# A retention layer whose queries and keys lose the norm's factor, with the order of its steps laid out anew

## The chip, the cores and the metric

The kernel runs on one core of a Trainium2 chip. The metric is the device time of one execution in microseconds (us). The engines have these short names: PE is TensorE (matmuls), DVE is VectorE, ACT is ScalarE, POOL is GpSimd and SP is SyncE, which here only issues transfers.

## The reference, cut to what matters

The program is a trunk of two layers over 512 tokens of 1024 features: a spatial gating layer, and a retention layer, each followed by a squared-ReLU MLP. The change is in the retention layer and the steps into and out of it.

```python
xn = x * rsqrt(mean(x * x) + EPS) * g
q, k, v, g = split(xn @ w_in)           # 4 heads; q, k: 256 wide, v, g: 512 wide
q, k = rotary(q, cos, sin), rotary(k, cos, sin) # k also scaled
o = (causal, decayed q k^T) v           # written as chunks with a state
o = rmsnorm(o, head_norm_g)             # per head and token
x = x + (o * silu(g)) @ w_out
```

Let r be a token's factor rsqrt(mean(x²) + EPS). Every projection is linear, so r can be applied to what comes out of it. The query's r multiplies a whole row of o, and the head norm divides such a factor out again, but for its EPS. The key's r can be moved into the value of the same token.

## The kernel before, in words

Each fp32 matmul is done as three products of split operands, high by high, high by low and low by high (`mm3`, L286). A weight piece is loaded by SP's queue (`load_part`, L169), cast to its high part by ACT (tile wH, L242) and lowered by DVE (wL, L249). `refill` (L268) casts three pieces ahead of PE and lowers two ahead. Two buffers hold loaded weights, with more in spare memory where there is some. A load waits for a free one.

The large products are done by `seven` (L467), a scheme of seven products of half sums in place of eight. It needs weights added to each other, which accumulating transfers on POOL's queue do (`add_up`, L213), and sums of the activations. `form` makes the sums: DVE makes sav from the whole h (hF), ACT casts it (spv, L613), DVE subtracts (spv, L616). There are seven products, each in two pieces of 12 matmuls, with the bank name in the tile: smva, smvb, smvc. A product's result is added to its place by DVE (L503) or copied there by ACT (L499, the first time). Bank a holds a running sum over several products, so the next product into it must wait for the addition of the one before. The values take 14 pieces, called v here; the gates g, and the second half of values and gates w and j. The sums of the first half are stored to DRAM (`keep_sums`, L1060; words k) and are fetched again for the second half by POOL's queue (`fetched`, L1065; tiles spx; words F).

The rope (`rope`, L1131) takes the two banks of a query or key of a head, makes six products and sums on DVE (tiles m) and splits them (qkH on ACT, qkL on DVE). Its tables, `rbc` and `r2bc`, are the two halves of tile wide. Before the change they are the cosines and sines times r: `norm("mix1")` makes r on POOL, `spread` (L360) puts it along all partitions by two diagonals on DVE and two matmuls (bc_mix), ACT copies it to wide (L371), and DVE multiplies both tables by it (L1243, L1244). Values take r in `split_v`, gates in `silu`. `av` (L1193) multiplies by the gate, squares, and takes the root of the head norm on POOL (rh); `turned` (words yt) transposes the result and splits it (ryH, ryL). The output products (words o and s) add it up.

The order of the steps is written out by hand in the text given to `play` (L1276). Each word is a step of PE (Q and q are queries and keys, v, g, w, j, o and s as above), and what stands in brackets behind it are the hooks that run in its step: f and F form sums, k stores them, R makes r, sc are scores, vs and si split values and gates, av and yt as above, w makes whole h, sq and ht prepare the next layer. Each engine runs its instructions in the order of issue, so a hook's place decides what stands behind what. 

Of the kernel before, what the change touches and what calls it, by code (L numbers as in the profile page):

```python
# [10 lines left out]
F32 = mybir.dt.float32  # L11
F32R = mybir.dt.float32r
I32 = mybir.dt.int32
AF = mybir.ActivationFunctionType
ALU = mybir.AluOpType
PSUM = bass.MemoryType.PSUM

P = 128
T = 512
D = 1024  # L20
KD = D // P
NT = T // P
# [4 lines left out]
DV = 512  # L27
EPS = 1e-6
# [60 lines left out]
def trunk(ctx, tc, x, norm_mix_g, norm_ffn_g, a_w_in, a_b_in, a_v_norm_g, a_w_s, a_b_s, a_w_out,  # L89
          b_w_in, b_head_norm_g, b_w_out, mlp_w1, mlp_w2, final_norm_g, trig, decay, out):  # L90
    nc = tc.nc
    ctx.enter_context(tc.manual_schedule())

    keep = ctx.enter_context(tc.tile_pool(name="keep", bufs=1))
# [9 lines left out]
    def big(shape, dt, name):  # L104
        return bigp.tile(shape, dt, tag="big", name=name)

    def tmp(name, tag, bufs=2):
        return work.tile([P, T], F32, tag=tag, name=name, bufs=bufs)

    def zt(name):  # L110
        return tmp(name, "z", 4)
# [7 lines left out]
    def f32(ap):  # L119
        return ap.bitcast(F32)  # L120
# [6 lines left out]
    gT = keep.tile([P, 80], F32, name="gT")  # L127
    wide = keep.tile([P, D], F32, name="wide")
    rbc, r2bc = wide[:, 0:T], wide[:, T:D]
    r4 = keep.tile([P, NT], F32, name="r4")  # L130
# [4 lines left out]
    mhalf = keep.tile([P, 2 * NT], F32, name="mhalf")  # L135
    mone = keep.tile([P, NT], F32, name="mone")
    r2s = keep.tile([P, 2, NT], F32, name="r2s")
# [1 line left out]
    ssh = keep.tile([P, H, NT], F32, name="ssh")  # L139
    msh = keep.tile([P, H, NT], F32, name="msh")  # L140
    rh = keep.tile([P, H, NT], F32, name="rh")
    keep.tile([P, 280], F32, name="fill")
    tok = [big([P, NT, 512], F32, f"tok{c}") for c in range(2)]
    hH, hL, hF = [None] * KD, [None] * KD, [None] * KD
    whole = [None, None]
# [16 lines left out]
    MIX, FFN, VG, HG, BU = 0, 16, 32, 48, 64  # L162
# [96 lines left out]
    def advance():  # L259
        for g in list(pending):  # L260
            if next(g, "end") == "end":
                pending.remove(g)
# [20 lines left out]
    def do(fn):  # L283
        step(lambda: fn())
# [7 lines left out]
    state = {}  # L292
# [21 lines left out]
    def chunk(k, ps, gcol):  # L314

        fresh_h(k, gcol)
        g = gT[:, gcol + k : gcol + k + 1]
        nc.scalar.activation(hH[k], ps, AF.Copy, scale=g)
        nc.vector.scalar_tensor_tensor(out=hL[k], in0=ps, scalar=g, in1=f32(hH[k]), op0=ALU.mult, op1=ALU.subtract)
# [30 lines left out]
        low.tensor_tensor(out=lo, in0=src, in1=f32(hi), op=ALU.subtract)  # L350
        return hi, lo

    def root(dst, power):

        a = work.tile([P, NT], F32, tag="ms", name="ms", bufs=2)
        nc.vector.tensor_tensor(out=a, in0=ssf[:, :, 0], in1=ssf[:, :, 1], op=ALU.add)
        nc.vector.tensor_scalar(out=a, in0=a, scalar1=1.0 / D, scalar2=EPS, op0=ALU.mult, op1=ALU.add)
        nc.gpsimd.tensor_tensor(out=dst, in0=a, in1=power[:, 0:NT], op=ALU.pow)

    def spread(src, dst, name):  # L360
# [12 lines left out]
    def norm(name):  # L373

        root(r4, mhalf)
        yield
        yield from spread(r4, rbc, name)
# [433 lines left out]
        return lambda kk, n: tuple(v[kk // 4][:, kk % 4, n * P : (n + 1) * P] for v in (h, l))  # L811

    late = {}

    def half_end(gcol):

# [11 lines left out]
    def late_chunks(gcol, ns):  # L828
        for k in range(4, KD):
            turn(late[k], k, ns)  # L830
        for k in range(4, KD):
            chunk(k, late[k], gcol)

    def nxt(g, times=1):
        return lambda: [next(g, None) for _ in range(times)]
# [242 lines left out]
    tV, form_v, prodV = zip(*[twofold(VW + 1024 * i, vF[i], sides[i], "vw"[i], (PLAN_V, PLAN_G)[i]) for i in range(2)])  # L1078
    tG, form_g, prodG = zip(*[twofold(GWT + 1024 * i, gF[i], sides[i], "gj"[i], PLAN_G, True) for i in range(2)])

    nrm1 = norm("mix1")
    LATE = MIX + 8

    def more0():
        do(lambda: extra.clear())

    def middle0(t):
        for k in (2 * t, 2 * t + 1):
# [18 lines left out]
    def gates(h):  # L1107
        return gF[h // 2][h % 2]

    def load_decay(h):  # L1110
        tab[h] = tmp(f"dec{h}", "ssq", 1)
        nc.sync.dma_start(out=tab[h], in_=decay[:, h, :])

    def split_v(h, ns):
        if 0 in ns:
            vv[h] = [big([P, NT, DV], F32R, f"vv{n}{h}") for n in "HL"]
        for n in ns:
            hi, lo, v = vv[h][0][:, n, :], vv[h][1][:, n, :], values(h)[:, n, :]
            assert {("unit", "vw"[h // 2], n // 2, h % 2), "r4"} <= ready, (h, n)
            ready.add(("v", h, n))  # L1120
            nc.scalar.activation(hi, v, AF.Copy, scale=r4[:, n : n + 1])
            nc.vector.scalar_tensor_tensor(out=lo, in0=v, scalar=r4[:, n : n + 1], in1=f32(hi), op0=ALU.mult, op1=ALU.subtract)

    def silu(h, ns):
        for n in ns:
# [5 lines left out]
    def rope(h, which, pa, pb):  # L1131
        cos, sin = rbc, r2bc
        if which == 0:
            qk[h] = (big([P, 4, T], F32R, f"qkH{h}"), big([P, 4, T], F32R, f"qkL{h}"))
        while "tab" not in state:
            yield
        m = [zt(f"m{h}{which}{i}") for i in range(4)]
        nc.vector.tensor_mul(m[0], pa, cos)
        nc.vector.tensor_mul(m[3], pa, sin)
        nc.vector.tensor_mul(m[1], pb, sin)  # L1140
        nc.vector.tensor_mul(m[2], pb, cos)
        nc.vector.tensor_sub(out=m[0], in0=m[0], in1=m[1])
        nc.vector.tensor_add(out=m[2], in0=m[2], in1=m[3])
        yield
        for i, mm in ((0, m[0]), (1, m[2])):
            hi, lo = qk[h][0][:, 2 * which + i, :], qk[h][1][:, 2 * which + i, :]
            nc.scalar.copy(out=hi, in_=mm)
            nc.vector.tensor_sub(out=lo, in0=mm, in1=f32(hi))
        ready.add(("qk", h, which))
# [43 lines left out]
    def av(h, n):  # L1193

        vhi, vlo = vv[h]
        ph, pl = pp[h]
        assert {(x, h, j) for x in "pv" for j in range(n + 1)} | {("g", h, n)} <= ready, (h, n)
        ps = mis(f"av{h}{n}")
        for j in range(n + 1):
            s = slice(POFF[j] + (n - j) * P, POFF[j] + (n - j + 1) * P)  # L1200
            mm3(ps, ph[:, s], pl[:, s], vhi[:, j, :], vlo[:, j, :], j == 0, j == n)

        def gen():
            y, ss, ms, r = gates(h)[:, n, :], ssh[:, h, n : n + 1], msh[:, h, n : n + 1], rh[:, h, n : n + 1]
            nc.vector.tensor_tensor(out=y, in0=ps, in1=y, op=ALU.mult)
            nc.scalar.activation(tmp(f"sqh{h}{n}", "sq"), ps, AF.Square, accum_out=ss)
            yield
            nc.vector.tensor_scalar(out=ms, in0=ss, scalar1=1.0 / DV, scalar2=EPS, op0=ALU.mult, op1=ALU.add)
            rsqrt(r, ms, 1)
            nc.scalar.activation(y, y, AF.Copy, scale=r)  # L1210
            ready.add(("y", h, n))
        launch(gen())
# [16 lines left out]
    rH, rL = {}, {}  # L1229

    def begin_values():
        tab["raw"] = [zt(f"trg{i}") for i in range(2)]
        for i in range(2):
            nc.sync.dma_start(out=tab["raw"][i], in_=trig[:, i, :])
        extra.clear()
        whole[:] = [None] * 2
        for k in range(4, KD):
            turn(late[k], k, (0,))

    def norm_ready():  # L1240
        assert state["R"] == 2
        next(nrm1, None)
        nc.vector.tensor_mul(r2bc, tab["raw"][1], rbc)  # L1243
        nc.vector.tensor_mul(rbc, tab["raw"][0], rbc)  # L1244
        state["tab"] = True
        load_decay(0)

    def out_pair(i, end=None):

# [7 lines left out]
    def act(word):  # L1257

        kind, nums = word.rstrip("0123456789"), [int(d) for d in word if d.isdigit()]
        return {  # L1260
            "R": lambda: (next(nrm1), ready.add("r4"), state.update(R=state.get("R", 0) + 1)),
            "N": norm_ready,
            "f": lambda: form_v[0](*nums),
            "k": lambda: keep_sums(*nums),
            "F": lambda: form_v[1](*nums),
            "sc": lambda: scores(*nums),
            "vs": lambda: split_v(nums[0], nums[1:]),
            "si": lambda: silu(nums[0], nums[1:]),
            "av": lambda: [(advance(), av(nums[0], n)) for n in nums[1:]],
            "yt": lambda: [turned(nums[0], c, acc if c > 1 else mis) for c in nums[1:]],  # L1270
            "sq": lambda: [tsq(n, 0) for n in nums if ready.issuperset({("ro1", 0)}) or 1 / 0],
            "ht": lambda: [turned_chunk(k, FFN + 8) for k in nums if ready.issuperset({("ro1", 0)}) or 1 / 0],
            "w": lambda: add_parts(*nums),
        }[kind]

    def play(script, **streams):  # L1276
# [17 lines left out]
    qs = [r for h in range(H) for r in qk_steps(h)]  # L1294
    do(begin_values)
    play("""
        Q(w1,w0,R) v v v v(f1,k1) v(R,N) v(f3) q q v(f4) v v(f5,k4) v v(k5) v v(k3) v +G g g g(sc00,sc01)
        g(sc02,sc03,vs00) g(vs01) g q g(vs02,vs03) g q g g g(si001) g(si02) q(si03,av03) q(av00,av02) g
        q(sc10,sc11,si10) g(av01,sc12) q(si12,si13,sc13,vs10123) q(yt00,si11,yt01) q(yt02,av101,F3) o(yt03,av123)
        o(yt10123) o(F4) +w o w o o w(F5) w o o w w w w w(F1) w w +j j w j w w(sc20) j w j(sc21,sc22) j(vs20) j(sc23)  # L1300
        q(vs22,vs23) j j(vs21) j q j(si21,si20,av21) q(si23,si22,av22,av20) q(av23) j(sc30,sc32) j(sc31)
        j(yt20123,vs3012) -(vs33,si301) j(sc33) s(si323,av30123) s(yt30123) s s s(sq0123,ht0) s(ht2,ht3) s(ht1)
    """, v=prodV[0], g=prodG[0], w=prodV[1], j=prodG[1], o=out_pair(0), s=out_pair(1, half_end(FFN + 8)),
        Q=qs[:1], q=qs[1:])
    may["extra"] = True
# [142 lines left out]
```

## Time and profile before

| what | us |
|---|---|
| time, median of 3 runs | 1342.58 (1342.38 to 1342.92) |
| the profiled execution's own time | 1342.99 |
| its span | 1341.3 |
| busy: PE | 1325.6 |
| busy: DVE | 798.5 |
| busy: ACT | 656.5 |
| busy: POOL | 126.8 |
| transfers | 213.88 MB, mean 159 GB/s |

The span is measured from the first to the last instruction. The mean granted clock of PE was 0.996 of full speed. PE's busy time includes modelled ends of matmuls, so what a matmul costs is read from the time between the starts of two in a row. The retention layer's PE work runs from about 615 to 1005 us of the span.

### The profile page before, as it was taken

To read this page: it belongs to the slowest core of one execution; us is meant where nothing else is said; L and a number is where in the kernel's file an instruction comes from. 1 tells how busy PE (TensorE), PEld (TensorE's weight loads), DVE (VectorE), ACT (ScalarE), POOL (GpSimd) and SP (SyncE) were. 2 spreads that over 40 slices of the span, in tenths; PEclk is the share of its full clock that TensorE was granted. 3 is DMA by queue.
4 is the path that set the end of the run, shared out by engine and by line. 5 is a ranking of instruction groups with operands and counts; after the bars stand their busy time and mean duration, and the time that the engine had idled before them with its cause. 6 is when DMAs were issued, how large, how long until landed. Compare 5 with 4: busy or idle time off the path is not lost.

```text
span 1341.3 us, 15169 instructions
## 1 busy us (share of the span) xinstructions
PE 1325.6 (99%) x6012; PEld 1099.9 (82%) x6012; DVE 798.5 (60%) x1005; ACT 656.5 (49%) x967; POOL 126.8 (9%) x113
## 2 busy tenths in 40 slices
PE   9999999999999999999899999999999999999997
PEld 7888888888888888888688888888888888888885
DVE  5664465342665655897966663556643565655697
ACT  5555443334444454655454452444634544444554
POOL 1000122000100001010100120101000000100003
PEclk9999999999999999999999999999999999999999
DMA  9661223234674758594987266963116575676763
GB/s 336 170 170 52 90 90 131 94 126 126 172 205 126 191 175 203 153 200 161 213 274 188 72 190 205 212 166 113 64 63 184 130 188 165 156 212 162 184 172 95
DMA packets 131352, 213.88 MB, mean 159 GB/s; under 512 B 3713, under 2 KB 56529, under 8 KB 130257
## 3 DMA queue, kind: packets, MB, share of 16 engines
q1 hardware_dynamic: 102928, 153.66, 33.2%
q0 software_dynamic: 28032, 58.72, 24.2%
q8 instruction: 47, 0.77, 0.2%
q10 hardware_dynamic: 320, 0.53, 0.1%
q14 instruction: 25, 0.20, 0.0%
HBM read 206.61 MB, written 6.29 MB: 159 GB/s over the span
## 4 chain that ended last, share of the span: by engine, by line
PE 94%; DVE 2%; ACT 2%; POOL 1%; issue 1%; ACTq 0%; POOLq 0%; DVEq 0%
PE up L289 24%; PE o L289 7%; PE u L289 6%; PE ro L289 6%; PE qk L289 5%; PE smwa L289 3%; PE v L875 2%; PE smga L289 2%; PE v L289 2%; PE sm01a L289 2%; PE smwc L289 2%; PE sm12a L289 2%; PE sm00a L289 2%; PE sm11a L289 2%; PE sm10a L289 2%; PE sm02a L289 2%
## 5 line engine op out<-in xcount | busy, mean ns | idle before, releaser
L249 DVE TENSOR_TENSOR wL<-raw,wH 128x1024 fp32r<-128x1024 f32 x265 | 324.6, 1229 | 200.1 <-issue 74.7
L242 ACT CAST wH<-raw 128x1024 fp32r<-128x1024 f32 x265 | 276.4, 1046 | 169.0 <-DMA raw<-in_b_w_in_dram 32.6
L289 PE MATMUL up<-hL,wH 128*128 128x512 f32 x480 | 186.9, 389 | 0.0
L289 PE MATMUL up<-hH,wH 128*128 128x512 f32 x480 | 186.9, 389 | 0.0
L289 PE MATMUL up<-hH,wL 128*128 128x512 f32 x480 | 186.9, 389 | 0.0
L976 ACT ACTIVATE aF<-up 128x512 f32<-128x512 f32 x60 | 36.0, 600 | 219.1 <-PE up L289 219.1
L289 PEld LDWEIGHTS up<-hH,wH 128*128 128x128 f32 x480 | 90.1, 188 | 18.8
L289 PEld LDWEIGHTS up<-hL,wH 128*128 128x128 f32 x480 | 90.2, 188 | 18.7
L289 PEld LDWEIGHTS up<-hH,wL 128*128 128x128 f32 x480 | 90.2, 188 | 18.5
L215 POOL DMA_DIRECT2D raw<-in_mlp_w_dram x29 | 37.9, 1366 | 500.0 <-DMA raw<-in_mlp_w_dram 201.0
L249 DVE TENSOR_TENSOR wL<-more,wH 128x1024 fp32r<-128x1024 f32 x42 | 51.2, 1220 | 52.6 <-issue 33.0
L616 DVE TENSOR_TENSOR sp<-aF,sp 128x512 fp32r<-128x512 f32 x48 | 31.0, 688 | 52.1 <-ACT sp L613 52.1
L242 ACT CAST wH<-more 128x1024 fp32r<-128x1024 f32 x42 | 43.9, 1045 | 20.9 <-PE sm00a L289 3.4
L289 PE MATMUL o<-wH,yH 128*128 128x512 f32 x128 | 51.0, 399 | 0.0
L289 PE MATMUL ro<-wH,ryH 128*128 128x512 f32 x128 | 50.7, 396 | 0.0
L289 PE MATMUL u<-hH,wH 128*128 128x512 f32 x128 | 50.3, 393 | 0.0
L289 PE MATMUL ro<-wH,ryL 128*128 128x512 f32 x128 | 50.1, 392 | 0.1
L289 PE MATMUL o<-wH,yL 128*128 128x512 f32 x128 | 50.0, 390 | 0.0
L289 PE MATMUL ro<-wL,ryH 128*128 128x512 f32 x128 | 49.9, 390 | 0.0
L289 PE MATMUL o<-wL,yH 128*128 128x512 f32 x128 | 49.9, 390 | 0.0
L289 PE MATMUL u<-hL,wH 128*128 128x512 f32 x128 | 49.9, 390 | 0.0
L289 PE MATMUL u<-hH,wL 128*128 128x512 f32 x128 | 49.9, 390 | 0.0
(462 smaller groups left out, 2841.9 us busy)
## 6 DMA issues: line engine op xcount, KB each, us to landing
raw<-in_mlp_w_dram SPq DMA_DIRECT2D x51, 1024.0 KB, 5.1
raw<-in_mlp_w_dram POOLq DMA_DIRECT2D x29, 1024.0 KB, 8.6
raw<-in_b_w_in_dram SPq DMA_DIRECT2D x28, 1024.0 KB, 5.3
more<-in_mlp_w_dram SPq DMA_DIRECT2D x21, 1024.0 KB, 5.0
raw<-in_b_w_in_dram POOLq DMA_DIRECT2D x16, 1024.0 KB, 10.7
raw<-in_a_w_in_dram SPq DMA_DIRECT2D x10, 1024.0 KB, 5.6
raw<-in_a_w_out_dram SPq DMA_DIRECT2D x8, 1024.0 KB, 4.9
raw<-in_b_w_out_dram SPq DMA_DIRECT2D x8, 1024.0 KB, 4.8
```

What stands on the lines that cost most here:

```text
L215: nc.gpsimd.dma_start(out=r.tile, in_=src, accum_op=ALU.add)
L242: nc.scalar.copy(out=p.hi, in_=p.src)
L249: nc.vector.tensor_sub(out=p.lo, in0=p.src, in1=f32(p.hi))
L289: nc.tensor.matmul(ps, lhsT=a, rhs=b, start=start and i == 0, stop=stop and i == 2, skip_group_check=resumed)
L616: nc.vector.tensor_sub(out=lo, in0=vs[c], in1=f32(hi))
L875: nc.tensor.matmul(accs0[n], lhsT=h[kk][:, n * P : (n + 1) * P], rhs=w, start=kk == 0 and j == 0, stop=kk == 7 and j == 2)
L976: nc.scalar.activation(a, ps, AF.Relu)
```

## The change

Queries and keys are used without r: the sines and cosines are loaded directly into wide, early (`load_trig`, called at the end of the first MLP), and the spread of r with its two matmuls, and the two products by it, are gone. Values get r² (`r2s`) where they got r, since they take the keys' r as well. The head norm's EPS becomes EPS times (mean(x²) + EPS) for each token (tile ea). `token_factors` makes r, r² and ea. Half of the whole h, the chunks 4 to 7, is made by four ACT activations straight from the banks (`late_chunks`) where `add_parts(1)` made it with four DVE additions (hook w1). The two lines of `play` below stand for the whole of the new text.

```diff
-    keep.tile([P, 280], F32, name="fill")
+    ea = keep.tile([P, NT], F32, name="ea")
+    keep.tile([P, 276], F32, name="fill")
...
+    def sum_squares():
         a = work.tile([P, NT], F32, tag="ms", name="ms", bufs=2)
         nc.vector.tensor_tensor(out=a, in0=ssf[:, :, 0], in1=ssf[:, :, 1], op=ALU.add)
         nc.vector.tensor_scalar(out=a, in0=a, scalar1=1.0 / D, scalar2=EPS, op0=ALU.mult, op1=ALU.add)
+        return a
...
             chunk(k, late[k], gcol)
+        if gcol == LATE:
+            whole[1] = big([P, 4, T], F32, "hF4")
+            for k in range(4, KD):
+                nc.scalar.activation(whole[1][:, k - 4, :], late[k], AF.Copy, scale=gT[:, gcol + k : gcol + k + 1])
...
-    nrm1 = norm("mix1")
-    LATE = MIX + 8
+    def load_trig():
+        for i, t in enumerate((rbc, r2bc)):
+            nc.sync.dma_start(out=t, in_=trig[:, i, :])
+        load_decay(0)
 
     def more0():
         do(lambda: extra.clear())
+        do(load_trig)
...
-            nc.scalar.activation(hi, v, AF.Copy, scale=r4[:, n : n + 1])
-            nc.vector.scalar_tensor_tensor(out=lo, in0=v, scalar=r4[:, n : n + 1], in1=f32(hi), op0=ALU.mult, op1=ALU.subtract)
+            r = r2s[:, 0, n : n + 1]
+            nc.scalar.activation(hi, v, AF.Copy, scale=r)
+            nc.vector.scalar_tensor_tensor(out=lo, in0=v, scalar=r, in1=f32(hi), op0=ALU.mult, op1=ALU.subtract)
...
-        while "tab" not in state:
+        while h == 0 and ("p", which) not in ready:
             yield
...
-            nc.vector.tensor_scalar(out=ms, in0=ss, scalar1=1.0 / DV, scalar2=EPS, op0=ALU.mult, op1=ALU.add)
+            nc.vector.tensor_scalar(out=ms, in0=ss, scalar1=1.0 / DV, scalar2=ea[:, n : n + 1], op0=ALU.mult, op1=ALU.add)
...
-        tab["raw"] = [zt(f"trg{i}") for i in range(2)]
-        for i in range(2):
-            nc.sync.dma_start(out=tab["raw"][i], in_=trig[:, i, :])
         extra.clear()
-        whole[:] = [None] * 2
+        whole[0] = None
...
-    def norm_ready():
-        assert state["R"] == 2
-        next(nrm1, None)
-        nc.vector.tensor_mul(r2bc, tab["raw"][1], rbc)
-        nc.vector.tensor_mul(rbc, tab["raw"][0], rbc)
-        state["tab"] = True
-        load_decay(0)
+    def token_factors():
+
+        a = sum_squares()
+        nc.vector.tensor_scalar(out=ea, in0=a, scalar1=EPS, scalar2=0.0, op0=ALU.mult, op1=ALU.add)
+        nc.gpsimd.tensor_tensor(out=r4, in0=a, in1=mhalf[:, 0:NT], op=ALU.pow)
+        nc.gpsimd.tensor_tensor(out=r2s[:, 0, :], in0=a, in1=mone, op=ALU.pow)
+        ready.add("r4")
...
-            "R": lambda: (next(nrm1), ready.add("r4"), state.update(R=state.get("R", 0) + 1)),
-            "N": norm_ready,
+            "R": token_factors,
+            "p": lambda: (ready.update(("p", n) for n in nums), advance()),
...
-        Q(w1,w0,R) v v v v(f1,k1) v(R,N) v(f3) q q v(f4) v v(f5,k4) v v(k5) v v(k3) v +G g g g(sc00,sc01)
...
+        Q v(w0) v(f1) v v v(p0,R,k1) v(f5) q q v(f4,f3) v v(p1) v(k3,k5) v v v +G v g g g(sc00) g(k4,sc03,vs00)
```

The new hook p0 or p1 lets the rope of head 0's queries or keys go on. What moves is seen best on the engines. DVE in the second half of the value products, up to the addition of what stands in bank a (vF<-smva, the last row), before; a wL is one weight piece, the m are the rope of head 0's keys, sav and spv a sum for a product:

```order
L249 TENSOR_TENSOR wL_4781<-raw_4635,wH_4780 128x1024
L599 TENSOR_TENSOR sav<-sav,hF_4547 128x512 x2
L616 TENSOR_TENSOR spv_4818<-sav,spv_4818 128x512 x2
L249 TENSOR_TENSOR wL_4815<-raw_4635,wH_4814 128x1024
L249 TENSOR_TENSOR wL_4838<-raw_4709,wH_4837 128x1024
L602 TENSOR_TENSOR sav<-hF_4552 128x512 x2
L616 TENSOR_TENSOR spv_4861<-sav,spv_4861 128x512 x2
L249 TENSOR_TENSOR wL_4858<-raw_4709,wH_4857 128x1024
L503 TENSOR_TENSOR vF_4723<-vF_4723,smvc_4649 128x512
L249 TENSOR_TENSOR wL_4883<-raw_4249,wH_4882 128x1024
L249 TENSOR_TENSOR wL_4903<-raw_4249,wH_4902 128x1024
L503 TENSOR_TENSOR vF_4723<-vF_4723,smva_4563 128x512
```

The same place after the change:

```order
L250 TENSOR_TENSOR wL_4818<-raw_4700,wH_4817 128x1024
L1152 TENSOR_TENSOR m_4841<-qk_4713,wide 128x512
L1154 TENSOR_TENSOR m_4842<-qk_4742,wide 128x512
L1156 TENSOR_TENSOR m_4841<-m_4841,m_4842 128x512
L1157 TENSOR_TENSOR m_4843<-m_4843,m_4844 128x512
L1162 TENSOR_TENSOR qkL_4554<-m_4841,qkH_4553 128x512
L250 TENSOR_TENSOR wL_4838<-raw_4700,wH_4837 128x1024
L508 TENSOR_TENSOR vF_4710<-vF_4710,smvc_4644 128x512
L250 TENSOR_TENSOR wL_4868<-raw_4254,wH_4867 128x1024
L250 TENSOR_TENSOR wL_4892<-raw_4254,wH_4891 128x1024
L508 TENSOR_TENSOR vF_4710<-vF_4710,smva_4555 128x512
```

The two sums' forming (rows 450, 451, 454 and 455) has moved ahead, and the rope of the keys has moved from ahead of these rows to between the two pieces of one weight tile, raw_4700.

The fetches of the stored sums on POOL, between the powers of the head norm (rh), before; sums_4645 is the sum of product 1, which the second half needs first:

```order
L336 TENSOR_TENSOR rh<-msh,mhalf 128x1 x2
L1069 DMA spx_5752<-sums_4942 128x2048
L336 TENSOR_TENSOR rh<-msh,mhalf 128x1 x2
L1069 DMA spx_5916<-sums_4868 128x2048
L1069 DMA spx_5950<-sums_4645 128x2048
L1069 DMA spx_6048<-sums_4906 128x2048
```

And after, where sums_4682 is the sum of product 1:

```order
L337 TENSOR_TENSOR rh<-msh,mhalf 128x1 x4
L1079 DMA spx_5873<-sums_4875 128x2048
L1079 DMA spx_5875<-sums_4873 128x2048
L1079 DMA spx_5933<-sums_5035 128x2048
L1079 DMA spx_5939<-sums_4682 128x2048
```

All four fetches now stand behind the four powers, and that of product 1 has moved from third to fourth place.

More of the change, by code (lines that the diff above doesn't have):

```diff
@@ L351, in split @@
         return hi, lo
-    def root(dst, power):
+    def sum_squares():
         a = work.tile([P, NT], F32, tag="ms", name="ms", bufs=2)
@@ L357, in root @@
         nc.vector.tensor_scalar(out=a, in0=a, scalar1=1.0 / D, scalar2=EPS, op0=ALU.mult, op1=ALU.add)
+        return a
+    def root(dst, power):
+        a = sum_squares()
         nc.gpsimd.tensor_tensor(out=dst, in0=a, in1=power[:, 0:NT], op=ALU.pow)
@@ L813, in trunk @@
     late = {}
+    LATE = MIX + 8
     def half_end(gcol):
@@ L1079, in trunk, with load_decay @@
     tG, form_g, prodG = zip(*[twofold(GWT + 1024 * i, gF[i], sides[i], "gj"[i], PLAN_G, True) for i in range(2)])
-    nrm1 = norm("mix1")
-    LATE = MIX + 8
+    def load_decay(h):
+        tab[h] = tmp(f"dec{h}", "ssq", 1)
+        nc.sync.dma_start(out=tab[h], in_=decay[:, h, :])
+    def load_trig():
+        for i, t in enumerate((rbc, r2bc)):
+            nc.sync.dma_start(out=t, in_=trig[:, i, :])
+        load_decay(0)
     def more0():
         do(lambda: extra.clear())
+        do(load_trig)
     def middle0(t):
@@ L1108, in gates @@
         return gF[h // 2][h % 2]
-    def load_decay(h):
-        tab[h] = tmp(f"dec{h}", "ssq", 1)
-        nc.sync.dma_start(out=tab[h], in_=decay[:, h, :])
     def split_v(h, ns):
@@ L1231, in begin_values @@
     def begin_values():
-        tab["raw"] = [zt(f"trg{i}") for i in range(2)]
-        for i in range(2):
-            nc.sync.dma_start(out=tab["raw"][i], in_=trig[:, i, :])
         extra.clear()
-        whole[:] = [None] * 2
+        whole[0] = None
         for k in range(4, KD):
             turn(late[k], k, (0,))
-    def norm_ready():
-        assert state["R"] == 2
-        next(nrm1, None)
-        nc.vector.tensor_mul(r2bc, tab["raw"][1], rbc)
-        nc.vector.tensor_mul(rbc, tab["raw"][0], rbc)
-        state["tab"] = True
-        load_decay(0)
+    def token_factors():
+        a = sum_squares()
+        nc.vector.tensor_scalar(out=ea, in0=a, scalar1=EPS, scalar2=0.0, op0=ALU.mult, op1=ALU.add)
+        nc.gpsimd.tensor_tensor(out=r4, in0=a, in1=mhalf[:, 0:NT], op=ALU.pow)
+        nc.gpsimd.tensor_tensor(out=r2s[:, 0, :], in0=a, in1=mone, op=ALU.pow)
+        ready.add("r4")
     def out_pair(i, end=None):
@@ L1296, in trunk @@
     play("""
-        Q(w1,w0,R) v v v v(f1,k1) v(R,N) v(f3) q q v(f4) v v(f5,k4) v v(k5) v v(k3) v +G g g g(sc00,sc01)
[L1298 to L1302, printed above, removed]
+        Q v(w0) v(f1) v v v(p0,R,k1) v(f5) q q v(f4,f3) v v(p1) v(k3,k5) v v v +G v g g g(sc00) g(k4,sc03,vs00)
+        g(sc02,vs03,sc01) g q(vs02) g g(vs01) q g(si01) g(si00) g g(av00) q q(si02) g(si03)
+        q(si10,sc10,sc11,si11,av02,av03,sc13) g(av01,sc12) q(si12,vs10123,yt00) q(yt03,si13,yt02,yt01) q(av101)
+        o(av123) o(yt10123,F5,F3) o +w o(F4) w o o w w o o w w w w w w +j w w j(F1,sc20) j w w(sc21) w j
+        j(sc22,vs20,vs22,sc23) j j(vs23) q j(vs21) j q j(si20) j(av20,si21,av21) q(si22,si23,av22) q(av23)
+        j(sc30,sc32,vs301) j(sc33,sc31) j(yt2012,si31) -(vs32,vs33) j(yt23,si30,av301) s(si323,av323) s(yt30123) s s
+        s(ht3) s(ht2,ht1) s(ht0,sq0123)
     """, v=prodV[0], g=prodG[0], w=prodV[1], j=prodG[1], o=out_pair(0), s=out_pair(1, half_end(FFN + 8)),
```

## The prediction, as put on record before the result

> **What bounds the kernel now.** I read the page's busy table first, then PE's waits, then the chain of waits around the stage that the change rewrites, then the granted clock there.
>
> ```profile
> PE 1325.6 (99%) x6012; PEld 1099.9 (82%) x6012; DVE 798.5 (60%) x1005; ACT 656.5 (49%) x967; POOL 126.8 (9%) x113
> ```
>
> TensorE (PE) is busy 99% of the span. So only two things can move the time: PE work that goes or comes, and the few microseconds in which PE stands still or runs slowly. PE's waits, over the whole span:
>
> ```profile
> PE smvc L289 <- DVE vF L503: 1.7, 1, 1.7
> PE smvc L289 <- ACT spv L613: 1.5, 1, 1.5
> PE qk L289 <- DVE m L1139: 0.7, 1, 0.7
> PE smja L289 <- DVE gF L503: 0.6, 1, 0.6
> ```
>
> The first three lie in one place, the products of the first values (tiles smva, smvb, smvc), where the change works. The chain of waits through it (start, us, engine, tile, line):
>
> ```profile
> 626.64 5.44 PE smva L289 x24
> ...
> 634.66 1.23 DVE wL L249
> ...
> 639.22 3.01 PE smvc L289 x12
> 642.23 0.24 PE bc_mix L369
> 642.47 0.25 PE bc_mix L370
> ...
> 644.08 0.70 DVE wide L1244
> 644.81 0.69 DVE m L1138
> 645.50 0.61 DVE m L1139
> 646.15 11.19 PE qk L289 x48
> ...
> 659.94 1.29 DVE qkL L1148 x2
> 661.24 1.14 DVE wL L249
> ...
> 671.90 10.88 PE smva L289 x48
> 682.78 0.23 PE smgc L289
> ```
>
> The reader is to see PE handing over to DVE three times. From 626.64 to 682.78 are 56.14 us. A row without a wait gives the price of a matmul: 48 in 10.88 us, 0.2267 us each. The stretch holds fourteen pieces of 12 and two of 24, 216 matmuls, 48.96 us. The two bc_mix rows add 0.49. So 6.69 us are loss, of which the waits name 1.7 + 0.7 + 1.5 = 3.9. Where some of the rest went, the windows by granted clock show (PEclk is the third figure from the right):
>
> ```profile
> 639.20:646.10 6.90, 6.23 (x26) 4.78 (x26) 5.56 (x10) 0.59 (x1) 0.00 (x0) 1.00 1.09 276
> 665.60:669.10 3.50, 3.50 (x10) 2.73 (x9) 3.43 (x4) 2.05 (x5) 0.00 (x0) 0.51 1.13 206
> ```
>
> Just after the 1.5 us wait, 3.5 us ran at clock 0.51: 3.5 x 0.49 = 1.7 us lost. After the 1.7 us wait before 639.22 the clock stayed at 1.00. Half-rate stretches thus followed one of the two long waits. The last 1.1 us lies in small pauses that I don't name.
>
> **What goes.** Queries and keys no longer need the norm's factor, so the two bc_mix matmuls (0.49) and, on DVE ahead of the first rope, two diagonals and the two wide products go. With them goes what made PE wait for m. Half of the whole h now comes from ACT instead of four DVE additions, 0.69 each by this row, and the row after it shows the stage's engines:
>
> ```profile
> L329 DVE TENSOR_TENSOR hF<-hH,hL 128x512 f32<-128x512 f32 x7 | 4.3, 690 | 0.0
> 626.60:682.80 56.20, 52.29 (x220) 41.82 (x219) 48.71 (x68) 27.34 (x37) 8.47 (x6) 0.97 0.88 244
> ```
>
> DVE is busy 48.7 of 56.2 us here and ACT 27.3, so four activations fit on ACT (at DVE's 0.69 each they are 2.8 us, the most that they could cost if PE stood behind all of them; I count nothing, since ACT is idle for half the stage). On DVE the four additions, two diagonals and two wide products are worth 8 x 0.69 = 5.5 us. Also the side for the third sum, spv1, is formed two steps sooner. I therefore count the start of smvc, the rope's wait, and the third wait in their old places all as gone: 6.69 + 0.49 = 7.18. The smja wait, 0.6, goes as well: a query step now stands between the two products that share a bank. Together **-7.8**.
>
> **Edits that I count at nothing.** One more power on POOL and one small DVE operation (ea), by these rows:
>
> ```profile
> 630.42 1.96 POOL L358 TENSOR_TENSOR r<-ms,mhalf 128x4 f32<-128x4 f32 x1 [35.95 <-DVE ms L357]
> L357 DVE TENSOR_SCALAR ms<-ms 128x4 f32<-128x4 f32 x1 | 0.2, 172 | 0.0
> ```
>
> POOL was idle for 35.95 us there, so 1.96 is hidden; it would cost that much only if an accumulate's issue stood behind it and was itself waited for. The 0.17 on DVE lies in a queue that lost 5.5. The trig loads and the first decay load move ahead on SP's queue into the end of the first MLP; a weight load behind them could land later by their time, but it is cast and lowered ahead of PE's need, and PE's waits name no weight load before as what they wait for. The stores of the sums only change places among each other.
>
> **What comes: the end of the value products.** The new order runs the rope of head 0's keys (six m, two qkL) later, between two halves (wL) of one weight tile, and the weight tile needs an accumulating transfer first. The rows of single transfers (us from issue to landing last): a plain load issued at 649.7, accumulating ones issued at 655.2 and, the slowest, at 657.8; and a weight cast:
>
> ```profile
> raw<-in_b_w_in_dram SPq DMA_DIRECT2D x1, 1024.0 KB, 4.9
> raw<-in_b_w_in_dram POOLq DMA_DIRECT2D x1, 1024.0 KB, 8.6
> raw<-in_b_w_in_dram POOLq DMA_DIRECT2D x1, 1024.0 KB, 18.9
> 660.41 1.05 ACT L242 CAST wH<-raw 128x1024 fp32r<-128x1024 f32 x1
> ```
>
> Counting DVE's new queue forward with the durations above, its slot comes free at about 646.05 (an estimate). Load 4.9, half a microsecond until POOL issues (a load issued at 649.7 landed at 654.6, its accumulate was issued at 655.2), accumulate 8.6: it lands at 660.2. Then DVE's queue, which stands behind it: cast 1.05, wL 1.23, the m 0.69 + 5 x 0.61, qkL 1.29, wL 1.23, two additions 1.29 (as the pair of qkL), two wL 1.23 + 1.14, and the addition that frees bank a, 0.69. That is 673.1. PE without a stall would want that bank at 626.64 + 16 pieces' worth, 192 x 0.2267 = 43.52, which is 670.2. PE waits **2.9**, some 1.2 before the twelfth piece for wL and 1.7 before the thirteenth for the bank. If the transfer is in time, DVE isn't late and it is 0; by the medians of the page, it is more:
>
> ```profile
> raw<-in_b_w_in_dram SPq DMA_DIRECT2D x28, 1024.0 KB, 5.3
> raw<-in_b_w_in_dram POOLq DMA_DIRECT2D x16, 1024.0 KB, 10.7
> ```
>
> That is 0.4 + 2.1 = 2.5 more, 5.4. I take 2.9, by the lone rows, since the new queue has one accumulate there at a time.
>
> **Three transposes in one hook** (yt03, yt02, yt01). Each puts one ryL on DVE ahead of the additions that free the small banks for av11 to av13:
>
> ```profile
> 782.75 1.29 DVE qkL L1148 x2
> ...
> 800.55 0.76 DVE ryL L1227
> ```
>
> I take one ryL that PE now sees, **0.8**. The bounds are nothing, if PE's query step hides it, and 0.76 + 1.29 = 2.0, if the rope's qkL stands in front as well.
>
> **The stored sums.** The second half of the values refetches four sums (spx) through POOL's queue, behind the power of av13. Call the end of that power T0: 796.78 + 1.46 = 798.24.
>
> ```profile
> 796.78 1.46 POOL L336 TENSOR_TENSOR rh<-msh,mhalf 128x1 f32<-128x1 f32 x1 [1.59 <-DVE msh L1208]
> 798.20 1.13 POOL L1069 DMA_DIRECT2D spx<-sums x2
> 801.20 0.53 POOL L1069 DMA_DIRECT2D spx<-sums x1 [1.87 <-ACT ryH L1226]
> ```
>
> ```profile
> 812.10 2.72 PE smwc L289 x12
> ```
>
> ```profile
> spx<-sums POOLq DMA_DIRECT2D x4, 1024.0 KB, 8.9
> spx<-sums POOLq DMA_DIRECT2D x1, 1024.0 KB, 5.1
> spx<-sums POOLq DMA_DIRECT2D x1, 1024.0 KB, 10.6
> ```
>
> ```profile
> 802.00:810.00 8.00, 8.00 (x37) 6.64 (x36) 4.91 (x6) 2.24 (x3) 0.00 (x0) 1.00 1.02 403
> ```
>
> Before, one sum was fetched ahead of T0 (POOL's order, shown above the prediction), and spx1, needed first, by smwc, was the third: by the row at 798.20, which holds two issues, it was issued at about 798.8, and with the slowest sum's 10.6 it landed at 809.4, 2.7 ahead of smwc at T0 + 13.9. Now all four are queued behind T0, and spx1 is the last. The queue is full at 403 GB/s, 2.6 us for a sum of 1.05 MB; the one fetched alone (789.9) took 5.1, so 2.5 go ahead. Four sums and one weight load: 2.5 + 5 x 2.6 = T0 + 15.5; with a second load T0 + 18.1. I take the middle, T0 + 16.6, and PE waits **2.7** (1.6 to 4.2). [...]
>
> **The clock.** Two of the new waits are 1.7 us or longer. One of two such waits was followed by 1.7 us lost. For the stretch by the smwc I count half of that, **+0.85**, and none for the other, at whose place DVE also waits (bounds 0 and 3.4).
>
> The sum against the profiled execution: -7.8 + 2.9 + 0.8 + 2.7 + 0.85 = -0.55 us. That execution took 1342.99 around a span of 1341.3, 0.4 over the median 1342.58; the sum is the same from either: 1342.58 - 0.55 = **1342.0 us**. About 0.2%, 2.7 us, is what a measurement of this kernel can tell from no change, so this is no change.
>
> **The rivals.** *Faster: the queues hold.* If the weight tile's accumulate lands before DVE comes to it, the 2.9 is gone, 1339.1; if also spx1 arrives in time, with 0.85 gone, 1335.6. For it: DVE loses 5.5 us of work in this very stage, and the reads of before show lone transfers landing in 4.9 and 8.6. Against it: the DMA share is above 1.00 in the windows shown. Chance 0.35.
>
> *Slower: spx1 lands like the slowest accumulate.* Issued last, near T0 + 3.0 (801.20), with 18.9 us to landing it is there at T0 + 21.9; smwc then waits 8.0 instead of 2.7, and a whole half-rate stretch follows, 1.7 instead of 0.85: +6.15, 1348.2. It decides from a landing later than T0 + 19.1: 1345.3 - 1342.0 is 3.3, less 0.85 for the clock leaves 2.5 over T0 + 16.6. For it: it is fourth in one queue, and the median of three was 8.9. Against: no stored sum took longer than 10.6. Chance 0.15.
>
> *No half-rate stretch.* [...] Chance 0.13. [...]
>
> *The change doesn't free the stage:* an earlier transfer, not DVE, holds smvc up, so 3 of the 7.8 stay: 1345. Against: the waits name DVE and ACT. It is in the range, and gets no more than the forecast's own spread.
>
> **How the numbers follow.** The forecast has 0.37; with the no-half-rate case, 0.13, that makes no change 0.50. The queues holding, 0.35, is faster; the late sum, 0.15, is slower. The range reaches down to both queues in time, 1335.6, and up to the forecast with the medians' 2.5 more at the value products and the clock's bound halfway between the 0.85 taken and 3.4 at most (1.7 more): 1342.05 + 2.5 + 1.7 = 1346.3. The late sum lies outside. The forecast's own range is 1340.0 to 1345.0.
>
> **What the profile after would show.** Right: no wait of smvc for vF or spv and no bc_mix; the waits list smva for DVE (wL, vF) at about 2.9 together around 670 us; smwc waits for a transfer, 2.7. Wrong: no wait above 0.5 at either place (the faster rival), or a wait of smwc over 5 us (the slower). A PEclk of 0.5 behind smwc or not decides the clock term. If smvc waits for something else at the old place, the 7.8 is wrong.

## The result, and the profile after

The changed kernel takes 1339.02 us, the median of 9 runs (1338.42 to 1340.75), against 1343.1 for the kernel before, median of 9 runs (1341.93 to 1343.38). The ratio is 0.9972, its 95% interval 0.9962 to 0.9982. Timed a second time it gave 1339.56 against 1343.12, ratio 0.9976 (0.9965 to 0.9986). So it is faster by 0.2 to 0.3%, about 3.6 to 4.1 us. The forecast was 1342.0 and no change; the range, 1335.6 to 1346.3, holds the result, but there is a small gain, which the forecast did not have.

The page's busy line of the profiled execution (span 1337.0 us) and PE's longest waits, to be set beside those of before (the wait of the program's first matmul, 1.4 us in both, and waits of 0.3 or less are not shown):

```profile
PE 1321.7 (99%) x6010; PEld 1097.7 (82%) x6010; DVE 794.4 (59%) x997; ACT 656.7 (49%) x969; POOL 126.9 (9%) x114
```

```profile
PE smwc L290 <- DMA spx<-sums: 1.9, 1, 1.9
PE smva L290 <- DVE vF L508: 1.4, 1, 1.4
PE smva L290 <- DVE wL L250: 0.9, 1, 0.9
```

DVE's busy time fell by 4.1 us (798.5 to 794.4), less than the 5.5 that the prediction took. None of the old waits of smvc, qk and smja is left in this list. The three that stand there are new: smva waits for wL and for vF, smwc for a stored sum. The chain of waits through the value products shows the stage in its new form:

```profile
626.26 5.44 PE smva L290 x24
...
637.14 0.14 issue
637.28 5.69 PE smvc L290 x24
642.97 10.88 PE qk L290 x48
...
659.29 5.44 PE smvc L290 x24
...
667.28 0.88 DVE wL L250
...
668.41 1.28 DVE vF L508 x2
669.69 2.27 DVE wL L250 x2
671.96 0.61 DVE vF L508
...
672.71 5.70 PE smva L290 x24
678.41 8.16 PE smgc L290 x36
```

From 626.26 to 678.41 are 52.15 us where there were 56.14: 4.0 less. PE hands nothing over from 626.26 to 667.24 but 0.14 us. Then it stands behind DVE in one chain: wL, two vF, two wL, vF. What DVE did just before that is in its timeline:

```profile
658.21 1.22 DVE L250 TENSOR_TENSOR wL<-raw,wH 128x1024 fp32r<-128x1024 f32 x1
661.16 1.23 DVE L250 TENSOR_TENSOR wL<-raw,wH 128x1024 fp32r<-128x1024 f32 x1 [1.73 <-ACT wH L243]
662.30 0.68 DVE L1152 TENSOR_TENSOR m<-qk,wide 128x512 f32<-128x512 f32 x1
```

DVE stood idle for 1.73 us until the weight was cast, and only then did the rope, from 662.30 to just ahead of the wL at 667.28, although PE had been done with the keys since 653.85, where the qk row ends. So the place of that rope is the first suspect, and the experiments test it. The stored sums, on POOL and in the chain of waits:

```profile
791.13 1.46 POOL L337 TENSOR_TENSOR rh<-msh,mhalf 128x1 f32<-128x1 f32 x1 [1.66 <-DVE msh L1222]
792.55 1.70 POOL L1079 DMA_DIRECT2D spx<-sums x3
796.38 0.54 POOL L1079 DMA_DIRECT2D spx<-sums x1 [2.13 <-ACT ryH L1240]
```

```profile
796.38 12.27 DMA spx<-sums
808.65 0.14 issue
808.79 3.00 PE smwc L290 x12
```

The last fetch of four is the one that PE needs first. It was issued at 796.38, landed after 12.27 us, and smwc began just behind it. The clock granted behind this wait and behind smva's was full:

```profile
808.80:814.00 5.20, 5.20 (x23) 4.30 (x24) 1.23 (x1) 1.06 (x1) 0.46 (x1) 1.00 0.52 202
672.70:680.00 7.30, 7.29 (x32) 6.07 (x33) 3.95 (x4) 4.91 (x6) 1.18 (x1) 1.00 1.01 409
```

### The profile page after: what moved, and what is told of

Read it like the earlier page. It is cut to its first block, busy times and chain, and to the rows that moved or that the text cites. A ratio compares the mean times of both kernels' runs of the same rounds, so it can differ in the third digit from the quotient of the medians.

```text
span 1337.0 us, 15157 instructions
## 1 busy us (share of the span) xinstructions
PE 1321.7 (99%) x6010; PEld 1097.7 (82%) x6010; DVE 794.4 (59%) x997; ACT 656.7 (49%) x969; POOL 126.9 (9%) x114
## 4 chain that ended last, share of the span: by engine, by line
PE 96%; DVE 1%; DMA 1%; ACT 1%; POOL 1%; issue 0%; ACTq 0%; POOLq 0%; DVEq 0%
PE up L290 24%; PE o L290 7%; PE u L290 7%; PE qk L290 6%; PE ro L290 6%; PE smwa L290 3%; PE av L290 2%; PE v L885 2%; PE smwc L290 2%; PE smga L290 2%; PE v L290 2%; PE sm12a L290 2%; PE sm11a L290 2%; PE sm10a L290 2%; PE sm02a L290 2%; PE sm01a L290 2%
```

## The experiments

The theory: what PE's waits name is what the kernel loses, each wait has one cause in the order of a queue, and they add up. The rivals are given with each run. In the text given to play, v is a step and p1 a hook.

**The changed kernel again** (after_again), unaltered, as the yardstick.

> The changed kernel, unaltered, as the yardstick for the other runs beside it. Theory (the waits add up: what the trace names as PE's waits is what the kernel loses): 1339.0 us, PE waits about 1.9 for a stored sum (smwc), 0.9 for wL and 1.4 for vF (smva), no half-rate stretch of the clock behind any of them. Rival (the clock's half-rate stretch comes and goes from run to run behind waits of 1.4 us and more): in this profile a stretch at about 0.5 stands behind one of the waits, and the time is up to 1.7 longer, 1340.7.

It took 1339.56 us. PE waited 2.1, 0.8 and 1.3. Behind the 2.1 the clock fell:

```profile
810.50:813.90 3.40, 3.40 (x10) 2.62 (x9) 0.99 (x1) 0.57 (x1) 0.00 (x0) 0.50 0.77 294
```

That is 3.4 us at 0.50, so 1.7 lost. The two profiles of this same kernel differ by 1338.8 - 1337.0 = 1.8 in their spans. The rival holds: the stretch comes and goes between executions of the same kernel.

**The stored sum of product 1 first** (f1_first).

```diff
-        o(av123) o(yt10123,F5,F3) o +w o(F4) w
+        o(av123) o(yt10123,F1,F5,F3) o +w o(F4) w
```

> The changed kernel with the stored sum of product 1 fetched first of the four instead of last. Theory (the order of the fetches decides): smwc no longer waits (at most 0.3), the time falls by the 2.0 us that were lost there, to 1337.0. Rival (the transfers together decide, so that the wait only moves to the next product that needs a sum, product 4, which is now fetched last): PE waits 1 to 2 us for spx at a later smw product, and the time stays at 1339.0 within 0.5.

Without the new F1, the fetch of this sum is issued by the product's own first step, behind the other three. It took 1337.04 us (5 runs, 1336.93 to 1337.47), ratio 0.9958 (0.9946 to 0.9971), 2.5 under the changed kernel beside it. The chain of waits runs through without a transfer:

```profile
796.60 10.98 PE ro L290 x48
807.58 2.72 PE smwc L290 x12
```

No wait moved to a later product. The theory holds: one place in POOL's queue cost 2 us, and it brought the chance of a half-rate stretch, as after_again has it.

**The keys' rope one piece earlier** (rope_early).

```diff
-        v(f4,f3) v v(p1) v(k3,k5)
+        v(f4,f3) v(p1) v v(k3,k5)
```

> The changed kernel with the rope of head 0's keys let go one value piece earlier, so that DVE does it while it waits for the accumulated weight tile. Theory (DVE's queue behind that tile is what makes smva wait): the 1.7 us that DVE stood idle before that tile's wL are filled, PE's waits there fall from 2.6 to about 0.9, the time falls by 1.6 to 1337.4. Rival (the rope then delays the split sums, spv, of the products before): a new wait of smva or smvc for spv of 1.5 us or more, the time is 1339.0 or more.

It took 1338.45 us, ratio 0.997 (0.9959 to 0.9982). DVE's timeline shows the idle time filled:

```profile
658.61 1.22 DVE L250 TENSOR_TENSOR wL<-raw,wH 128x1024 fp32r<-128x1024 f32 x1
659.75 0.69 DVE L1152 TENSOR_TENSOR m<-qk,wide 128x512 f32<-128x512 f32 x1
...
664.72 2.36 DVE L250 TENSOR_TENSOR wL<-raw,wH 128x1024 fp32r<-128x1024 f32 x2
```

PE's waits in this place fell from 0.9 and 1.4 to one of 1.1, and no wait for spv came up. The median fell by 1.1 against the changed kernel beside it and by 0.6 against its first timing, less than the forecast 1.6; its runs spread from 1337.79 to 1340.43, and the intervals of the two ratios overlap, so the time alone doesn't settle it. The waits do.

**The changed arithmetic in the old order** (old_order). The text of play is that of before, with these words replaced:

```diff
-        Q(w1,w0,R) v v v v(f1,k1) v(R,N)
+        Q(w0,R) v v v v(f1,k1) v(p01)
```

> The changed arithmetic (no factor in queries and keys, half of whole h from the banks) in the old order of steps and hooks; only the hooks that no longer exist are replaced. Theory (algebra and order each bring a part): the two matmuls (0.5) and the rope's wait (0.7) go, and DVE's 5.5 us less shorten the two smvc waits (1.7 and 1.5) by half; smja's 0.6 stays and smwc does not wait, since the old order of fetches is back; 1343.1 - 0.5 - 0.7 - 1.6 = 1340.3, and 1.7 less if the half-rate stretch goes. Rival (the order alone brings the gain): no more than the two matmuls and the rope's wait, 1341.9. Second rival (the algebra alone brings it): 1337, lower than the changed kernel, for the waits that the new order adds are missing too.

It took 1341.39 us, ratio 0.9988 (0.9979 to 0.9997): 1.7 of the gain. So the algebra in the old order brings a part, and the new order on top of it the rest; the new order without the algebra was not run. But the waits are not as I expected:

```profile
PE smvc L290 <- DVE vF L508: 1.7, 1, 1.7
PE smvc L290 <- ACT spv L618: 1.5, 1, 1.5
PE smja L290 <- DVE gF L508: 1.1, 1, 1.1
PE smva L290 <- DVE vF L508: 0.6, 1, 0.6
```

The two waits of smvc are what they were, 1.7 and 1.5, with 4.3 us less work on DVE (busy 794.2, against 798.5 before). That the waits would shorten by half was wrong. Only the wait of qk for m is gone, and smva has a new one of 0.6. The two matmuls and the 0.7, less this 0.6, leave 0.6 us for the algebra in this stage. The rest of the 2.2 us by which the stage is shorter here (53.9, from 56.14) is about the 1.7 us of the half-rate stretch, which this profile doesn't have. Whether the algebra removed it, or it only fell out here, is not shown.

**Old order, with one sum formed sooner** (old_f1). Against old_order:

```diff
-        Q(w0,R) v v v v(f1,k1) v(p01)
+        Q(w0,R) v v(f1) v v(k1) v(p01)
```

> The changed arithmetic in the old order, with one hook moved: the split sum of product 1 (f1) is formed two value pieces sooner, as in the new order. Theory (the place of that sum's work in DVE's queue, ahead of the addition that frees smvc's bank, is what made smvc wait, not the amount of DVE's work): the 1.7 us wait of smvc for vF goes down to 0.3 or less, the 1.5 for spv stays, the time is 1341.4 - 1.6 = 1339.8. Rival (the wait is set by the weights' lowering): it stays at 1 or more, time 1341 or more.

It took 1339.69 us, ratio 0.9973 (0.9963 to 0.9983), 1.7 under old_order. The 1.7 us wait is gone, the 1.5 stands. DVE's timeline shows why: the additions from smvb now follow PE and not the sum's spv:

```profile
631.43 1.29 DVE L621 TENSOR_TENSOR spv<-sav,spv 128x512 fp32r<-128x512 f32 x2
...
635.82 0.69 DVE L508 TENSOR_TENSOR vF<-vF,smvb 128x512 f32<-128x512 f32 x1 [0.29 <-PE smvb L290]
637.18 0.69 DVE L508 TENSOR_TENSOR vF<-vF,smvb 128x512 f32<-128x512 f32 x1 [0.67 <-PE smvb L290]
```

The place of one sum in the queue made the wait, not DVE's load.

**Old order, with only the keys' rope in its new place** (old_p1). Against old_order:

```diff
-        v(p01) v(f3) q q v(f4) v v(f5,k4)
+        v(p0) v(f3) q q v(f4) v v(f5,k4,p1)
```

> The changed arithmetic in the old order, with the keys' rope alone moved to its new place. Theory (the rope stood ahead of the split sum for the second smvc and made it wait; behind, it stands ahead of the addition that frees bank a, together with the split sum of product 5, which the old order forms late): smvc's 1.5 us wait for spv is gone, but smva now waits 4 to 5 us in all, 2.4 as in the changed kernel plus 2.6 for that sum; time 1341.4 - 1.7 - 0.6 + 5.0 = 1344.1. Rival (each move gains by itself): the 1.5 goes and smva waits 2.4 as in the changed kernel, 1341.4 or less.

It took 1343.65 us, 2.3 more than old_order (2.7 by the two ratios, since they were timed beside different runs of before), ratio to before 1.0008 (0.9999 to 1.0016). The 1.5 is gone, and smva waits instead:

```profile
PE smva L290 <- DVE wL L250: 3.5, 1, 3.5
PE smvc L290 <- DVE vF L508: 1.7, 1, 1.7
PE smva L290 <- DVE vF L508: 1.4, 1, 1.4
```

3.5 + 1.4 = 4.9 us, within the 4 to 5 expected. DVE's timeline has the sum of product 5, up to 666.55, and then the rope ahead of the weight that smva waits for:

```profile
665.34 1.29 DVE L621 TENSOR_TENSOR spv<-sav,spv 128x512 fp32r<-128x512 f32 x2 [0.69 <-ACT spv L618]
666.55 0.69 DVE L1152 TENSOR_TENSOR m<-qk,wide 128x512 f32<-128x512 f32 x1
...
671.52 1.22 DVE L250 TENSOR_TENSOR wL<-raw,wH 128x1024 fp32r<-128x1024 f32 x1
```

So the moves do not each gain by themselves: in the old order the rope's new place loses, with this sum ahead of it. The new order forms the sum earlier; that this is enough to make the rope's place pay was not run by itself. (In the first listing of DVE's order in the section on the change, this sum is the row L602 and the L616 behind it. The row numbers 450 to 455, named below that listing, mean these two rows and the L599 and L616 above them.)

**Half of the whole h on DVE again** (dve_whole). The four activations in late_chunks are left out, and:

```diff
-        Q v(w0) v(f1)
+        Q(w1) v(w0) v(f1)
```

> The changed kernel with chunks 4 to 7 of the whole h made by four DVE additions, hung on the first query's step, as before, and not by ACT from the banks. Theory (DVE is idle for 1.1 and 1.8 us just ahead of there, so that part of the 2.4 us is hidden): the start of smvc waits about 0.6 more, time 1339.9. Rival (all of DVE's saved work counts): smvc waits 2.4 more, time 1341.7. Second rival (it counts for nothing): within 0.3 of the changed kernel.

It took 1339.86 us, ratio 0.9978 (0.9969 to 0.9987): 0.3 to 0.8 over the changed kernel's two medians, which the intervals can't separate. Its waits name 0.6 for smvc behind vF, where the changed kernel has 0.14:

```profile
PE smvc L290 <- DVE vF L508: 0.6, 1, 0.6
```

The four additions are 2.5 us of DVE's busy time (796.9, against 794.4 in the changed kernel), and some 0.5 of that reach PE.

**Both repairs** (both_early): the edits of f1_first and rope_early together.

> The changed kernel with both repairs: the stored sum of product 1 fetched first, and the keys' rope let go one value piece earlier. Theory (the waits add up): no wait of smwc for spx, one of about 1.1 for wL at smva, no other above 0.5; time 1339.3 - 2.2 - 1.3 = 1335.8. Rival (a wait removed early comes back later, since the transfers then stand closer to their use): smwc or a later product waits 1 us or more for a transfer, the time is 1337 or more.

It took 1335.95 us (5 runs, 1335.57 to 1336.71), ratio 0.9946 (0.9933 to 0.996). It beats both kernels. PE's waits behind the start of the program are down to these and 0.2 of yt:

```profile
PE smva L290 <- DVE wL L250: 0.6, 1, 0.6
PE smva L290 <- DVE vF L508: 0.3, 1, 0.3
PE smgc L290 <- DVE wL L250: 0.3, 1, 0.3
```

The repairs add up.

**The rope four pieces later** (both_late), with the sum first:

```diff
-        v(f4,f3) v v(p1) v(k3,k5) v v v +G v
+        v(f4,f3) v v v(k3,k5) v v(p1) v +G v
```

> The changed kernel with the stored sum of product 1 fetched first and the keys' rope let go four value pieces later, behind the last products of the first values. Theory (DVE's queue behind the late weight tile is what makes smva wait, and the rope has no one waiting for it before the first scores): both waits of smva are gone (each at most 0.3), no half-rate stretch can follow, time 1339.3 - 2.2 - 2.4 = 1334.7. Rival (the rope's two banks are then held too long): the first gate products, smgc, wait 1 us or more for DVE's m, or the first scores for qkL, and the time is 1336 or more.

A miss: 1341.39 us, ratio 0.9988 (0.9979 to 0.9997), and smva waits 4.4 us for vF. A hook runs ahead of the additions of its own step, so the rope stood exactly ahead of the addition that frees bank a:

```profile
668.32 2.36 DVE L250 TENSOR_TENSOR wL<-raw,wH 128x1024 fp32r<-128x1024 f32 x2 [2.43 <-ACT wH L243]
670.60 0.68 DVE L1152 TENSOR_TENSOR m<-qk,wide 128x512 f32<-128x512 f32 x1
...
674.19 1.28 DVE L508 TENSOR_TENSOR vF<-vF,smva 128x512 f32<-128x512 f32 x2
```

PE's first 4.3 us of work behind the wait ran at half the clock, so that 2.2 us were lost; the 24 matmuls of smva took 7.80 us there, against 5.70 in the changed kernel:

```profile
675.10:679.40 4.30, 4.30 (x10) 3.40 (x11) 2.80 (x4) 3.03 (x4) 0.00 (x0) 0.50 1.03 432
```

**The rope one piece further** (both_behind), behind these additions:

```diff
-        v(f4,f3) v v(p1) v(k3,k5) v v v +G v
+        v(f4,f3) v v v(k3,k5) v v v(p1) +G v
```

> As the kernel with both repairs, but the keys' rope is let go one piece later than in the run before, so that it stands on DVE behind the additions into bank a and not ahead of them. Theory (what stood ahead of the addition that frees bank a was the 4.4 us wait, the six m and nothing else): smva waits less than 0.4, the time is 1336.0 - 0.9 = 1335.1 where the gate products do not wait. Rival (the rope now stands ahead of the gates' weight tiles): smgc waits 1.5 us or more for wL, the time is 1336.5 or more.

A miss again, 1340.96 us, ratio 0.9984 (0.9975 to 0.9993). The rival came true, and the theory's 4.4 fell only to 1.4:

```profile
PE smgc L290 <- DVE wL L250: 3.4, 2, 3.1
PE smva L290 <- DVE vF L508: 1.4, 1, 1.4
```

The rope now stands between the two halves of the gates' weight tile, whose accumulate had taken 21.0 us to land. And without any rope ahead of it, smva still waits 1.4, for DVE was idle before the wL that stands ahead of the additions:

```profile
669.04 2.36 DVE L250 TENSOR_TENSOR wL<-raw,wH 128x1024 fp32r<-128x1024 f32 x2 [2.83 <-ACT wH L243]
671.32 1.28 DVE L508 TENSOR_TENSOR vF<-vF,smva 128x512 f32<-128x512 f32 x2
```

So the weight tile two pieces on is late too: ACT stood idle for 4.19 us until its accumulate landed, and cast it from 667.95. In the changed kernel ACT casts this tile from 667.05, and the first wL could have followed the cast of 1.05 at about 668.1 (an estimate); behind the rope it came at 669.6, some 1.5 us later. So both the rope and the transfer have a part in smva's second wait there. Their exact shares are not settled; that the early rope leaves 0.6 + 0.3 (both_early) or 1.1 (rope_early) is measured.

**The kernel before again** (before_again), for one more profile. The clock's window in the expectation is 3.413 us, the length of the half-rate stretch in the clock's records of the first profile of before.

> The kernel before, unaltered, for one more profile. Theory (the half-rate stretch depends on when in the clock's window a wait falls, not on the kernel): the waits of PE are the same 1.7, 1.5, 0.7 and 0.6 as in the first profile; a stretch near 0.5 stands behind the 1.5, behind the 1.7 or behind none; without it the span is 1.7 shorter than 1341.3. Rival (it belongs to the 1.5 us wait): again just behind that wait.

It took 1343.39 us, span 1341.7. The waits were 1.7, 1.5, 0.7 and, at smja, 1.1. The half-rate stretch stood again behind the 1.5:

```profile
664.80:668.60 3.80, 3.80 (x11) 2.95 (x11) 3.80 (x5) 2.63 (x4) 0.00 (x0) 0.55 1.13 207
```

That speaks for the rival. But old_order has the same wait of 1.5 at nearly the same place, and no such stretch:

```profile
663.00:669.00 6.00, 5.98 (x25) 4.66 (x26) 5.31 (x7) 4.55 (x8) 0.00 (x0) 1.00 1.13 207
```

So neither pure form holds. What the clock's records add to this stands in the last section.

## Why the prediction was right in its places and off in its sizes

**What goes, -7.8.** Right in its places, 0.9 us too large. The stage lost its named waits, the half-rate stretch and bc_mix. The smja wait went, too. But the stage is 4.0 us shorter with 2.3 us of new waits in it, so 6.3 went where 7.18 was taken: the last 1.1 us, the small pauses that the prediction didn't name and yet counted as gone, stayed for the most part (52.15 - 48.96 - 2.3 = 0.9). The reason given for smvc was half wrong: I put DVE's lighter load beside the earlier sum. old_order has the first without the second, and both waits stayed; old_f1 has the second, and the 1.7 went. The 1.5 went when the keys' rope no longer stood ahead of the sum that smvc needs (old_p1), a reason that the prediction doesn't give. The wait of qk for m is the only one that the algebra itself removed, with the two matmuls.

**The value products, +2.9.** Right in place and cause. The accumulate landed 8.4 us after its issue (8.6 taken). The waits are 0.9 + 1.4 = 2.3 where 1.2 + 1.7 stood.

**Three transposes, +0.8.** Wrong: no wait there; the waits name 0.2 at a yt, for pm. The bound of nothing was the true one.

**Stored sums, +2.7.** Right mechanism, smaller size: the power ended at 791.13 + 1.46 = 792.59 and the sum landed at 808.65, T0 + 16.1 where 16.6 was taken. PE waited 1.9, and f1_first shows that the place in the queue made the wait. (The middle of the prediction's 15.5 and 18.1 is 16.8, not 16.6; by that the wait would have been 2.9.) From 794 to 808 us the queues moved 370 GB/s on average (after), where the prediction took the 403 of a shorter stretch of before.

**The clock, +0.85.** Nothing in the first profile, 1.7 in the second: a term that is a draw, not a size. That the first profile had none is luck.

The last four terms came out 0.6 + 0.8 + 0.8 + 0.85 = 3.05 us below what was taken, and the first 0.9 short. Together the named places give -6.9 + 2.3 + 1.9 = -2.7 us. The spans of the two profiles differ by 4.3 us (1341.3 and 1337.0), the medians by 4.1. The other 1.6 us lie where the prediction has no term: some 0.4 ahead of the stage (it begins at 626.64 and 626.26), 0.9 between the stage and the smwc (129.3 us before, 128.5 after without the wait), and the rest behind. What made them is not shown, and the medians of the kernel before differ among themselves by 0.5 (1342.58 and 1343.1).

So the forecast of no change failed in the sizes of its terms, in one wait that did not exist, at the transposes, and in taking nothing for the rest of the program. The range held all this because it reached down to the case of both queues in time, which is not what happened: that is luck in part. (For the clock's part of the range's upper end, halfway between 0.85 and 3.4 is 1.3 more and not 1.7, which makes 1345.8; the result is far from there.)

Of the rivals, "no half-rate stretch" was what the profiled run did, with the clock at 1.00 behind a wait of 1.9 us, while after_again had a stretch behind a wait of 2.1 us; "the queues hold" was wrong, since both queues waited as forecast; "spx1 lands like the slowest accumulate" did not come, 12.27 against 18.9. That the change doesn't free the stage did not come either.

## What to carry to other kernels

Where PE is busy 99%, count a change by the waits at named places, not by the work that it takes off another engine: 4.3 us less on DVE moved neither of two waits (old_order), while one hook moved by two steps removed 1.7 us (old_f1). Look at what an engine's queue holds ahead of the one instruction that PE waits for: an addition that frees a bank, or a fetch that is needed first. And when a new order is predicted, a wait that follows from one late transfer can be placed well and sized within 0.8 us, as here, while a small one that only could occur, like that of the transposes, is best kept at nothing with its price in the range.

## What the runs showed of the hardware

PE ran at half the clock behind a wait in four profiles: behind 1.5 us in before and before_again, behind 2.1 in after_again and behind 4.4 in both_late. The clock stayed at 1.00 behind a wait of 1.9 us in after (808.80 to 814.00) and behind one of 1.5 in old_order (663 to 669). Behind the 3.1 us of both_behind there was no such stretch either: 23 matmuls took 5.54 us, 0.24 each. So the length of the wait alone doesn't decide it.

The clock's records of before and after have a length in common. In before the half-rate stretch lasts 3.413 us, from 665.63 to 669.05, and the full clock ahead of it 658.77 us, which is 193 times 3.4133. In after the clock is full for 1324.37 us, 388 times 3.4133, up to 1329.91, behind the last matmul. If the time is cut into windows of this length, counted from the start of each profile's first record (6.86 in before, 5.54 in after), the wait of 1.5 us in before lies whole in the window just ahead of the stretch. A line between two windows cuts the 1.7 in before into 0.8 and 0.9, and the 1.9 of after into 0.8 and 1.1, and no stretch followed either. None followed the 1.4 of after, which lies whole in one window. So the place of a wait in these windows fits why the changed kernel had the stretch in one execution and not in the other, but that is not shown, and what exactly trips the clock stays open.

f1_first, which has waits of 0.9 and 1.4 us only, has closely spaced times: 1336.93 to 1337.47 in 5 runs, against 1338.73 to 1341.62 in 8 runs of the changed kernel beside it. That no half-rate stretch follows these waits would be a reason, but is not shown.
